# Choosing experts beside the gate tables: a re-staged slot schedule, 8-token one-hot compares, and the gate factor on ScalarE

## The chip, the core and the metric

The kernel runs on one core of one Trainium2 chip. The metric is the device time of one execution in microseconds (us); three runs of the kernel before gave 2725.94, 2727.11 and 2727.88, so the median is 2727.11. The engines are PE (TensorE), DVE (VectorE), ACT (ScalarE), POOL (GpSimd) and SP (SyncE, which here only issues transfers). Each has its own queue of instructions and takes them in order.

## What is computed

Two transformer blocks on 512 tokens of width 1024. The change lies in the expert layer that ends the first block. For every token and each of 8 heads, 16 of 16384 experts are chosen by two top-16 lists (one for each half of a key) and a top-16 over their sums; the expert's number is `i1 * 128 + i2`. In the reference:

```python
v1, i1 = lax.top_k(s1, PEER_TOPK_HALF)
v2, i2 = lax.top_k(s2, PEER_TOPK_HALF)
cand = (v1[..., :, None] + v2[..., None, :])...
top_s, pos = lax.top_k(cand, PEER_TOPK)
gate = jax.nn.softmax(top_s, axis=-1)
u = jnp.take(expert_u, experts, axis=0)
act = jax.nn.gelu(jnp.einsum('chkd,cd->chk', u, hc))
v = jnp.take(expert_v, experts, axis=0)
return jnp.einsum('chk,chkd->cd', gate * act, v)
```

## The kernel before

For the last 128 tokens the kernel gathers the chosen rows of `expert_u` and `expert_v` (128 choices of each) and works on them on DVE: "picks". For the first 384 tokens (tiles t = 0, 1, 2 of 128) it computes all 16384 experts densely in 128 blocks of 128, block i being one value of `i1`: a **U main** is `expert_u` block i times the activations (8 chunks of 3 matmuls, 128x384), gelu on ACT, and a store to a scratch tensor `asc`; a **V main** later multiplies gelu and gate with `expert_v` block i. Both split each weight block into a high part (`uhi`, an ACT copy, L100) and a remainder (`ulo`, a subtraction, L101).

The gate of every token and expert is a table built as a product of one-hot matrices: for each token, `ob` (128 choices x 128 values of i2) and `oa` (128 choices x 128 values of i1, times the gate) are multiplied on PE. `gate_rows` makes `ob` and `oa` for a **unit** of TB = 8 tokens, `gate_mm` multiplies them (8 products) into two PSUM banks and copies them to a staging tile `st`, which holds TG tokens. A full `st` is written to the scratch tensor `gsc` in 8 **pieces**. The V stage reads the table back (`vg`). 384 tokens are 48 units.

All of this is written under a hand-made order, in **slots**. Slot i issues the load of U block i+3, `u_prep(i+2)` (`uhi` on ACT, then `ulo` on the engine in `gb["ulo"]`), the caller's work for DVE, the U main i, the caller's `gate_mm`, gelu i, some pieces and some picks. Before the change the slots run in two stages one after the other:

- 25 slots with the choices (`choose`, a generator with seven parts, six of them each ahead of a slot) for the gathered tile and then tiles 0, 1, 2. `ulo` is on POOL here.
- 56 slots with the gates: seven units in eight slots, one pick in each. `ulo` is on DVE here. `gate_mm` of a unit runs in the slot after its `gate_rows`.

Five slots drain the pieces and two bridge to the U/V stage, where the last 40 blocks' U mains (U blocks 88 to 127) run among the 128 V mains. `choose` ends with an Exp on ACT (L611), which takes a change of the activation table and, at the next gelu, another. Buffers that matter: `uhi`, `ulo` and `uraw` three each, `ob` and `oa` two each, gate PSUM five banks, U main PSUM two.

Of the kernel before, what the change touches and what calls it, by code (L numbers as in the profile page):

```python
# [7 lines left out]
F32 = mybir.dt.float32  # L8
# [4 lines left out]
AF = mybir.ActivationFunctionType  # L13
ALU = mybir.AluOpType
# [6 lines left out]
P = 128  # L21
# [4 lines left out]
TD = 384  # L26
NH = 8
NE = 128
TB = 8
OB = 2  # L30
NTAP = 7
WINDOWS = (8, 15, 16, 17)
UPS = (7, 8)
TG = 64
IB = 16
CPICK, CGAP = (0, 1, 0, 0, 1, 0, 0), (1,)
BPICK, BDRAIN = 1, 2
BRIDGE = 2
MASK = -1.0e30
# [20 lines left out]
def body(nc, tc, A, out, stop=None):  # L60
# [23 lines left out]
    iotaf = const.tile([P, P], F32, name="iotaf")  # L84
# [193 lines left out]
    start = tc.manual_schedule()  # L278
# [17 lines left out]
    ps = lin.bank()  # L296
# [13 lines left out]
    first = [lin.bank() for _ in range(8)]  # L310
    H = []
    for k in range(DC):
        if k + 2 < DC:
            load(k + 2)
        h = tmp.tile([P, S], F32, tag="ht", name="ht", bufs=2)
# [7 lines left out]
        for m in range(8):  # L323
            j = m % 2 * P
# [36 lines left out]
    steps = [(mg, k0) for mg in order1 for k0 in (0, 4)]  # L361
# [19 lines left out]
    for i, (mg, k0) in enumerate(steps):  # L381
# [7 lines left out]
        if k0 == 0:  # L389
            ps = [lin.bank() for _ in range(2)]  # L390
# [21 lines left out]
    for c in range(4):  # L412
        ps = lin.bank()
# [4 lines left out]
                                       op1=ALU.subtract)  # L418
# [11 lines left out]
    ps = fsum(lin.bank(), ycv)  # L430
# [53 lines left out]
    GT = TD // P  # L484
# [8 lines left out]
    vvs = ExitStack()  # L493
# [199 lines left out]
        nc.scalar.copy(gb["t3"], pt)  # L693

    def gate_rows(t, q):
        if q == 0:
            gate_t(t)
        t3 = gb["t3"]
        ob = gp.tile([P, TB, P], F32, tag="ob", name="ob", bufs=OB)
        oa = gp.tile([P, TB, P], F32, tag="oa", name="oa", bufs=OB)  # L700
        for j in range(TB):
            of = lambda n: t3[:, n, q * TB + j:q * TB + j + 1]
            nc.vector.tensor_scalar(ob[:, j], iotaf, of(1), None, op0=ALU.is_equal)
            nc.vector.tensor_scalar(oa[:, j], iotaf, of(0), of(2), op0=ALU.is_equal, op1=ALU.mult)
        return t, q, ob, oa

    def gate_mm(t, q, ob, oa):

        g, o = divmod(t * P + q * TB, TG)
        if o == 0:  # L710
            gb["st"] = gp.tile([P, P, TG], F32, tag="st", name="st", bufs=2)
        for h in range(TB // 4):
            ps = pg.tile([P, 4, P], F32, tag="pg", name="pg", bufs=5)
            for j in range(4):
                nc.tensor.matmul(ps[:, j], ob[:, 4 * h + j], oa[:, 4 * h + j], start=True, stop=True)
            nc.scalar.copy(gb["st"][:, :, o + 4 * h:o + 4 * h + 4].rearrange("p i t -> p t i"), ps)
        if o + TB == TG:
            for b in range(NE // IB):
                pieces.append((Gsc[b][g], gb["st"][:, b * IB:(b + 1) * IB].rearrange("p i t -> p (i t)")))
# [12 lines left out]
    ui = 0  # L732

    def slot(dve=None, after=None, picks=0, drain=1):
        nonlocal ui
        i = ui
        ui += 1
        if i + 3 < NE:
            u_load(i + 3)
        u_prep(i + 2)  # L740
        r = dve() if dve else None
        u_main(i)
        if after:
            after()
        u_post(i, True)
        piece(drain)
        pick(picks)
        return r

    for n, t in enumerate([GT] + list(range(GT))):  # L750
        for n2, _ in enumerate(choose(t)):
            slot(picks=CPICK[n2] if n > 1 or n == 1 and n2 > 1 else 0)
    for n in CGAP:
        slot(picks=n)
    tk.close()
    vvs.close()
    gs = ExitStack()
    gp = R(gs, "gp")
    pg = pool(gs, "pg", 1, space=PSUM)
    units = [(t, q) for t in range(GT) for q in range(P // TB)]  # L760
    ready = []
    nu = 0
    first = ui
    gb["ulo"] = nc.vector
    while nu < len(units) or ready:
        mine = []
        want = (ui - first + 1) * UPS[0] // UPS[1]
        old, ready = ready, []

        def dve():  # L770
            nonlocal nu
            while nu < min(want, len(units)):
                ready.append(gate_rows(*units[nu]))
                nu += 1

        def after():
            for o in old:
                gate_mm(*o)
        slot(dve, after, 1)
    while pieces:  # L780
        slot(picks=BPICK, drain=BDRAIN)
    gs.close()
    gb["ulo"] = nc.gpsimd


# [8 lines left out]
    def v_load(i):  # L794
        raw = vp.tile([P, D], F32, tag="vraw", name="vraw", bufs=4)
        nc.sync.dma_start(raw, A["v"][i * P:(i + 1) * P, :])
        a = None
        kind = "s" if i in Asc else "d"
        if i % 2 == 0:
            VG[kind] = vp.tile([P, TD // TG, 2, TG], F32, tag=f"vg{kind}", name="vg", bufs=2 + (kind == "s"))  # L800
            o = i % IB * TG
            nc.sync.dma_start(VG[kind].rearrange("p g i t -> p g (i t)"),
                              Gsc[i // IB][:, :, o:o + 2 * TG].rearrange("g p n -> p g n"))
        g = VG[kind][:, :, i % 2]
        if i in Asc:
            a = vp.tile([P, TD], F32, tag="va", name="va", bufs=4)
            nc.sync.dma_start(a, Asc[i])
        V[i] = raw, g, a
# [23 lines left out]
                    hi[:, s2 * S:(s2 + 1) * S], lo[:, s2 * S:(s2 + 1) * S], nv == 0, nv == NE - 1)  # L832
        nv += 1

    if (ui + BRIDGE) % 2:
        slot(picks=BPICK)
    direct = list(range(ui + BRIDGE, NE))
    spilled = list(range(ui + BRIDGE))
# [420 lines left out]
```

## Time and profile before

| what | value |
|---|---|
| median of three runs | 2727.11 us (2725.94 to 2727.88) |
| the profiled execution | 2732.3 us, span 2730.5 us |
| PE, busy share of the span | 95% (weight loads 79%) |
| DVE / ACT / POOL | 72% / 36% / 29% |
| mean granted clock of TensorE | 0.977 |
| U mains 0 to 27 (choices) | 444.5 to 612.1 us |
| U mains 28 to 81 (gates) | to 923.2 us |
| U mains 82 to 87 (drain and bridge) | to 952.4 us |
| the U/V stage | to about 1660 us |
| DVE at the last top-16 lists of the query stage | to 455.8 us |

Busy times count an instruction from start to end; instructions of one engine overlap by a tenth of a microsecond or so, so the time that a run of them takes is read from start to start. A wait in brackets is the idle time of the engine just before the instruction and the instruction that ended it. PEclk is the granted clock, 1.0 being 2.4 GHz and 0.5 being 1.2 GHz.

### The profile page before, as it was taken

What the parts mean: (1) busy time and instruction counts of PE and PEld (TensorE: products, weight loads), DVE (VectorE), ACT (ScalarE), POOL (GpSimd) and SP (SyncE); (2) the same over time, 40 slices, a digit from 0 to 9 for tenths busy, and PEclk for the clock granted to TensorE, in tenths of its full rate; (3) what the DMA queues carried; (4) which work ended last, traced back from release to release, by engine and by line L of the source; (5) the groups of instructions that cost most, each with busy time, mean ns of one, the idle gap of its engine ahead of it and who ended that gap; (6) DMA issues with size and microseconds to landing.
All of it is one profiled execution on the core that took longest, in us unless ns stands there. A gap on an engine that the chain in (4) does not pass through costs nothing. (4 is left out here: it accounts for less than half of the span.)

```text
span 2730.5 us, 33539 instructions
## 1 busy us (share of the span) xinstructions
PE 2583.6 (95%) x12307; PEld 2153.1 (79%) x12307; DVE 1956.9 (72%) x3659; ACT 985.5 (36%) x1374; POOL 790.5 (29%) x455
## 2 busy tenths in 40 slices
PE   6988899769999999999999999999999999999998
PEld 4766679769999988887887887778888775788886
DVE  6999578999999688888888888644334475544433
ACT  3324333325555433333333335222232455422221
POOL 0000333542222377777777764000010000100000
PEclk8998999979999999999999999999999999999999
DMA  8434321437878899898989994222333221222232
GB/s 291 148 123 162 133 70 58 149 134 256 306 269 320 324 343 320 318 323 311 318 313 315 319 326 175 85 93 93 94 99 104 85 89 39 85 93 93 94 95 73
DMA packets 205061, 508.05 MB, mean 186 GB/s; under 512 B 18208, under 2 KB 94496, under 8 KB 204896
## 3 DMA queue, kind: packets, MB, share of 16 engines
q1 hardware_dynamic: 154928, 354.18, 37.6%
q0 software_dynamic: 36864, 134.23, 13.9%
q10 hardware_dynamic: 13104, 17.50, 1.8%
q8 instruction: 97, 1.59, 0.2%
q14 instruction: 68, 0.56, 0.1%
HBM read 461.23 MB, written 44.61 MB: 185 GB/s over the span
## 5 line engine op out<-in xcount | busy, mean ns | idle before, releaser
L101 DVE TENSOR_TENSOR wlo<-raw,whi 128x1024 fp32r<-128x1024 f32 x212 | 258.8, 1223 | 339.2 <-ACT whi L100 334.6
L100 ACT CAST whi<-raw 128x1024 fp32r<-128x1024 f32 x228 | 235.1, 1034 | 659.6 <-PE mm L105 547.5
L106 PE MATMUL act<-h2h,ulo 128*128 128x384 f32 x1024 | 348.8, 341 | 33.0 <-POOL ulo L101 25.6
L104 PE MATMUL act<-h2h,uhi 128*128 128x384 f32 x1024 | 351.8, 344 | 16.4 <-ACT ga L650 16.4
L105 PE MATMUL mm<-gl,whi 128*128 128x512 f32 x864 | 345.2, 400 | 3.6 <-DVE gl L208 3.5
L105 PE MATMUL act<-h2l,uhi 128*128 128x384 f32 x1024 | 347.2, 339 | 0.0
L104 PE MATMUL mm<-gh,whi 128*128 128x512 f32 x864 | 343.1, 397 | 0.4 <-DVE x L887 0.4
L106 PE MATMUL mm<-gh,wlo 128*128 128x512 f32 x864 | 342.0, 396 | 1.5 <-DVE wlo L101 1.5
L179 POOL TENSOR_TENSOR sq<-sq 128x512 f32<-128x512 f32 x24 | 37.0, 1542 | 960.9 <-ACT sq L173 960.3
L104 PE MATMUL pv<-vhi,ch 128*128 128x512 f32 x768 | 301.2, 392 | 7.2 <-ACT ch L821 7.2
L106 PE MATMUL pv<-vhi,cl 128*128 128x512 f32 x768 | 307.1, 400 | 0.0
L105 PE MATMUL pv<-vlo,ch 128*128 128x512 f32 x768 | 301.9, 393 | 5.3 <-POOL vlo L822 5.3
L680 POOL DMA_INDIRECT row<-in_u_dram,idx x128 | 185.3, 1448 | 297.3 <-DVE act L663 282.9
L106 PEld LDWEIGHTS act<-h2h,ulo 128*128 128x128 f32 x1024 | 195.8, 191 | 37.8 <-POOL ulo L101 29.8
L101 POOL TENSOR_TENSOR ulo<-uraw,uhi 128x1024 fp32r<-128x1024 f32 x68 | 193.1, 2842 | 100.9 <-ACT uhi L100 100.4
L104 PEld LDWEIGHTS act<-h2h,uhi 128*128 128x128 f32 x1024 | 196.0, 191 | 18.9 <-ACT ga L650 17.3
L671 DVE SCALAR_TENSOR_TENSOR gacc<-row,act,gacc 128x1024 f32<-128x1024 f32 x127 | 205.4, 1618 | 3.4 <-DMA row<-in_v_dram,idx 1.9
L105 PEld LDWEIGHTS mm<-gl,whi 128*128 128x128 f32 x864 | 162.5, 188 | 44.4 <-DVE gl L208 4.9
L105 PEld LDWEIGHTS act<-h2l,uhi 128*128 128x128 f32 x1024 | 196.1, 191 | 1.5
L104 PEld LDWEIGHTS mm<-gh,whi 128*128 128x128 f32 x864 | 162.4, 188 | 43.0 <-issue 2.3
L106 PEld LDWEIGHTS mm<-gh,wlo 128*128 128x128 f32 x864 | 162.5, 188 | 41.8 <-issue 2.0
L663 DVE CUSTOM_DVE_ANT_0 row<-row,h2t 128x1024 f32<-128x1024 f32 x128 | 178.4, 1405 | 13.2 <-DMA row<-in_u_dram,idx 13.2
(826 smaller groups left out, 5242.7 us busy)
## 6 DMA issues: line engine op xcount, KB each, us to landing
uraw<-in_uT_dram SPq DMA_DIRECT2D x128, 512.0 KB
vraw<-in_v_dram SPq DMA_DIRECT2D x128, 512.0 KB
raw<-in_w_in_dram SPq DMA_DIRECT2D x52, 512.0 KB
gsc<-st SPq DMA_DIRECT2D x48, 512.0 KB
vg<-gsc SPq DMA_DIRECT2D x64, 384.0 KB
raw<-in_ffn_w_gate_dram SPq DMA_DIRECT2D x44, 512.0 KB
raw<-in_ffn_w_up_dram SPq DMA_DIRECT2D x44, 512.0 KB
raw<-in_ffn_w_down_dram SPq DMA_DIRECT2D x40, 512.0 KB
```

Source lines behind the costliest of these rows:

```text
L100: nc.scalar.copy(hi, src)
L101: (lo_eng or nc.vector).tensor_sub(lo, src, hi.bitcast(F32))
L104: nc.tensor.matmul(ps, whi, ahi, start=first, stop=False)
L105: nc.tensor.matmul(ps, whi, alo, start=False, stop=False)
L106: nc.tensor.matmul(ps, wlo, ahi, start=False, stop=last)
L179: self.eng.tensor_add(self.acc, self.acc, t)
L663: nc.vector.tensor_tensor_reduce(out=r, in0=r, in1=h2t, scale=1.0, scalar=0.0, op0=ALU.mult, op1=ALU.add, accum_out=act[:, k:k + 1])
L671: nc.vector.scalar_tensor_tensor(gb["acc"], r, act[:, k:k + 1], gb["acc"], op0=ALU.mult, op1=ALU.add)
L680: nc.gpsimd.indirect_dma_start(out=r, out_offset=None, in_=A[table], in_offset=bass.IndirectOffsetOnAxis(ap=idx[:, k:k + 1], axis=0))
```

## The change

Five things are altered.

1. Choices and gates run in one loop of 82 slots (n = 0 to 81). The choices of the gathered tile and of tile 0 take two parts in every three slots up to n = 20; those of tiles 1 and 2 take one part in every third slot from n = 23 to 62. Units start at n = 22, three in four slots, and from n = 62 nine in ten. A tile's units wait in the program until its choice is complete. `ulo` is on DVE in all of the loop.
2. `gate_rows` makes `ob` and `oa` with one compare each for all 8 tokens (operands broadcast), not with 16 operations of one token; the gate factor is then multiplied into `oa`, in place, by 8 ACT operations of 128x128 with a per-partition scale.
3. `gate_mm` writes its products into PSUM with the token as the innermost index (each matmul's 128 columns lie 16 bytes apart), so that the copy to `st` reads the bank in order and writes runs of 4 values, where it wrote single values 256 bytes apart.
4. `st` holds 32 tokens, not 64: 96 pieces of 256 KB with up to two issued in a slot, where there were 48 of 512 KB with one. `vg` is loaded for four blocks at a time (768 KB), not two (384 KB), with two buffers of each kind.
5. Fewer picks ahead of the U/V stage: 58 rather than 67. The number of slots ahead of it stays 86 and two of the bridge.

```diff
-UPS = (7, 8)
-TG = 64
+TG = 32
+GI = 4
 IB = 16
-CPICK, CGAP = (0, 1, 0, 0, 1, 0, 0), (1,)
...
         ob = gp.tile([P, TB, P], F32, tag="ob", name="ob", bufs=OB)
         oa = gp.tile([P, TB, P], F32, tag="oa", name="oa", bufs=OB)
+        k0 = q * TB
+        shape = [P, TB, P]
+        row = lambda n: t3[:, n, k0:k0 + TB, None].to_broadcast(shape)
+        cols = iotaf[:, None, :].to_broadcast(shape)
+        nc.vector.tensor_tensor(ob, cols, row(1), op=ALU.is_equal)
+        nc.vector.tensor_tensor(oa, cols, row(0), op=ALU.is_equal)
         for j in range(TB):
-            of = lambda n: t3[:, n, q * TB + j:q * TB + j + 1]
-            nc.vector.tensor_scalar(ob[:, j], iotaf, of(1), None, op0=ALU.is_equal)
-            nc.vector.tensor_scalar(oa[:, j], iotaf, of(0), of(2), op0=ALU.is_equal, op1=ALU.mult)
+            nc.scalar.activation(oa[:, j], oa[:, j], AF.Copy, scale=t3[:, 2, k0 + j:k0 + j + 1])
         return t, q, ob, oa
...
         for h in range(TB // 4):
-            ps = pg.tile([P, 4, P], F32, tag="pg", name="pg", bufs=5)
+            ps = pg.tile([P, P, 4], F32, tag="pg", name="pg", bufs=5)
             for j in range(4):
-                nc.tensor.matmul(ps[:, j], ob[:, 4 * h + j], oa[:, 4 * h + j], start=True, stop=True)
-            nc.scalar.copy(gb["st"][:, :, o + 4 * h:o + 4 * h + 4].rearrange("p i t -> p t i"), ps)
+                nc.tensor.matmul(ps[:, :, j], ob[:, 4 * h + j], oa[:, 4 * h + j], start=True, stop=True)
+            nc.scalar.copy(gb["st"][:, :, o + 4 * h:o + 4 * h + 4], ps)
...
-    for n, t in enumerate([GT] + list(range(GT))):
-        for n2, _ in enumerate(choose(t)):
-            slot(picks=CPICK[n2] if n > 1 or n == 1 and n2 > 1 else 0)
-    for n in CGAP:
-        slot(picks=n)
-    tk.close()
-    vvs.close()
...
+    gens = [choose(t) for t in torder]
     ready = []
-    nu = 0
-    first = ui
+    steps = nu = n = 0
     gb["ulo"] = nc.vector
     while nu < len(units) or ready:
-        mine = []
-        want = (ui - first + 1) * UPS[0] // UPS[1]
+        csteps = 2 * (n + 1) // 3 if n < 21 else min(28, 14 + (n - 20) // 3)
+        want = max(0, (n - 20) * 3 // 4) if n < 62 else 32 + (n - 62) * 9 // 10
         old, ready = ready, []
 
         def dve():
-            nonlocal nu
-            while nu < min(want, len(units)):
+            nonlocal nu, steps
+            while steps < csteps:
+                next(gens[steps // 7], None)
+                steps += 1
+            while nu < min(want, len(units), max(0, steps // 7 - 1) * (P // TB)):
                 ready.append(gate_rows(*units[nu]))
                 nu += 1
...
-        slot(dve, after, 1)
+        slot(dve, after, 0 if n < 11 or n % 4 == 3 and n < 62 or n % 3 != 2 and n < 21 else 1, 2)
+        n += 1
     while pieces:
         slot(picks=BPICK, drain=BDRAIN)
...
-            VG[kind] = vp.tile([P, TD // TG, 2, TG], F32, tag=f"vg{kind}", name="vg", bufs=2 + (kind == "s"))
...
+            vg = VG[kind, i // GI] = vp.tile([P, TD // TG, GI, TG], F32, tag=f"vg{kind}", name="vg", bufs=2)
...
-    if (ui + BRIDGE) % 2:
+    while (ui + BRIDGE) % GI:
         slot(picks=BPICK)
```

The queue of ACT before, in the middle of the gate stage (`uhi`: split of a U block; `st<-pg`: copy of a gate bank; `ga`: gelu; `asc`: store of it):

```order
L100 CAST uhi<-uraw 128x1024
L716 COPY st<-pg 128x4x128 x2
L650 ACTIVATE ga<-act 128x384
L654 DMA asc_6867<-ga 128x384
L100 CAST uhi<-uraw 128x1024
```

The same queue now, in a slot of the loop that has a unit and follows one that has (`oa<-oa`: the gate factor), up to the next split:

```order
L99 CAST uhi<-uraw 128x1024
L708 ACTIVATE oa<-oa,t_5608 128x128 x8
L720 COPY st<-pg 128x128x4 x2
L649 ACTIVATE ga<-act 128x384
L653 DMA asc_5759<-ga 128x384
L99 CAST uhi<-uraw 128x1024
```

Between the split of one block and the split of the next, eight operations on this slot's `oa` now stand ahead of the copies of the unit before.

The queue of DVE before, in the gate stage (`row`, `act`: a pick; `ob`, `oa` stand here once of eight times on either side):

```order
L704 TENSOR_SCALAR oa<-iotaf,t_4664 128x128
L663 ISA row,act<-row,h2t 128x1024
L663 ISA act 128x1
L101 TENSOR_TENSOR ulo<-uraw,uhi 128x1024
L703 TENSOR_SCALAR ob<-iotaf,t_4664 128x128
L704 TENSOR_SCALAR oa<-iotaf,t_4664 128x128
```

The same queue now, in a slot that has a unit and a part of the choices (`x`, `I_3307`: that part):

```order
L100 TENSOR_TENSOR ulo<-uraw,uhi 128x1024
L562 TENSOR_TENSOR x<-x 128x128x8
L562 TENSOR_TENSOR x<-x 128x128x4
L562 TENSOR_TENSOR x<-x 128x128x2
L563 TENSOR_TENSOR I_3307<-x 128x128
L599 TENSOR_TENSOR x<-ge,starts 128x2048
L705 TENSOR_TENSOR ob<-iotaf,t_4325 128x1024
L706 TENSOR_TENSOR oa<-iotaf,t_4325 128x1024
L662 ISA row,act<-row,h2t 128x1024
L662 ISA act 128x1
L100 TENSOR_TENSOR ulo<-uraw,uhi 128x1024
```

The remainder `ulo` comes first, then the part of the choices, then the two compares, then the pick.

## Rows read from the trace of the kernel before

**Rows 1.** Windows by stage: length, busy PE, PEld, DVE, ACT, POOL, PEclk, DMA, GB/s

```profile
444.50:612.10 167.60, 128.71 (x694) 126.26 (x693) 162.76 (x481) 56.05 (x72) 78.06 (x32) 0.88 0.42 137
612.10:923.20 311.10, 311.10 (x2072) 311.10 (x2072) 296.11 (x917) 172.82 (x207) 87.20 (x55) 1.00 0.80 282
...
952.40:1660.00 707.60, 686.54 (x3156) 575.70 (x3155) 611.72 (x558) 239.13 (x326) 512.03 (x290) 1.00 0.91 320
```

**Rows 2.** Waits from 444.5 to 612.1: waiting, releaser, us in total, times, longest

```profile
ACT ex L611 <- DVE ex L585: 31.9, 3, 12.8
...
PE act L106 <- POOL ulo L101: 16.7, 3, 15.5
```

**Rows 3.** Timeline of PE in the gate stage: start, us, engine, line, operation, tiles

```profile
709.78 1.95 PE L715 MATMUL pg<-oa,ob 128*128 128x128 f32 x16
711.48 0.42 PE L104 MATMUL act<-h2h,uhi 128*128 128x384 f32 x1
...
717.43 0.42 PE L104 MATMUL act<-h2h,uhi 128*128 128x384 f32 x1
```

**Rows 4.** Timeline of PE: first matmuls of U mains 2 and 3, back to back

```profile
454.71 0.33 PE L104 MATMUL act<-h2h,uhi 128*128 128x384 f32 x1
...
458.87 0.33 PE L104 MATMUL act<-h2h,uhi 128*128 128x384 f32 x1
```

**Rows 5.** Timeline of DVE through one slot of the gate stage

```profile
703.17 1.21 DVE L663 CUSTOM_DVE_ANT_0 row<-row,h2t 128x1024 f32<-128x1024 f32 x1
...
704.31 1.22 DVE L101 TENSOR_TENSOR ulo<-uraw,uhi 128x1024 fp32r<-128x1024 f32 x1
...
705.45 0.28 DVE L703 TENSOR_SCALAR ob<-iotaf,t 128x128 f32<-128x128 f32 x1
...
709.07 1.21 DVE L663 CUSTOM_DVE_ANT_0 row<-row,h2t 128x1024 f32<-128x1024 f32 x1
```

**Rows 6.** Timelines of DVE (the choice of tile 2) and of POOL

```profile
572.62 0.29 DVE L570 CAST IF<-II 128x256 bf16<-128x256 uint32 x1
...
587.56 3.12 DVE L595 TENSOR_TENSOR x<-x,IF 128x2048 bf16<-128x2048 bf16 x1
...
603.40 0.29 DVE L619 TENSOR_TENSOR GA<-ex,sm 128x128 f32<-128x128 f32 x1
...
584.56 5.05 POOL L101 TENSOR_TENSOR ulo<-uraw,uhi 128x1024 fp32r<-128x1024 f32 x2
```

**Rows 7.** Timelines of ACT: two gate copies; gelu and the next split; a table load

```profile
664.75 2.03 ACT L716 COPY st<-pg 128x512 f32<-128x512 f32 x2 [2.07 <-PE pg L715]
...
521.37 0.50 ACT L650 ACTIVATE ga<-act 128x384 f32<-128x384 f32 x1 [2.16 <-PE act L106]
...
522.32 1.06 ACT L100 CAST uhi<-uraw 128x1024 fp32r<-128x1024 f32 x1 [0.45 <-ACT ga L650]
...
530.59 1.28 ACT L611 ACT_TABLE_LOAD   x1 [0.40 <-ACT ga L650]
```

**Rows 8.** Timelines of ACT and DVE: a split, and the remainder that waited for it

```profile
927.69 1.05 ACT L100 CAST uhi<-uraw 128x1024 fp32r<-128x1024 f32 x1 [4.00 <-DMA uraw<-in_uT_dram]
...
928.77 1.23 DVE L101 TENSOR_TENSOR ulo<-uraw,uhi 128x1024 fp32r<-128x1024 f32 x1 [4.33 <-ACT uhi L100]
```

**Rows 9.** Timelines of ACT: a 128x128 operation and its successor; a 128x512 copy and its

```profile
2183.76 0.40 ACT L1078 ACTIVATE s__17856<-s__17856,st__17857 128x128 f32<-128x128 f32 x1 [0.40 <-DVE st__17857 L1077]
2184.07 0.19 ACT L1078 ACTIVATION_READ_ACCUMULATOR s__17856<-s__17856,st__17857 128x1 f32 x1
...
418.46 0.59 ACT L537 COPY q<-mm 128x512 f32<-128x512 f32 x1 [3.89 <-PE mm L106]
418.95 1.05 ACT L100 CAST whi<-raw 128x1024 fp32r<-128x1024 f32 x1
```

**Rows 10.** Timeline of PE: the matmul after an idle time, and one 3.5 us later

```profile
57.37 0.79 PE L105 MATMUL mm<-hl,whi 128*128 128x512 f32 x1 [2.62 <-DVE hl L196]
...
60.87 0.40 PE L104 MATMUL mm<-hh,whi 128*128 128x512 f32 x1
```

More of the change, by code (lines that the diff above doesn't have):

```diff
@@ L782, in body @@
     gs.close()
+    tk.close()
+    vvs.close()
     gb["ulo"] = nc.gpsimd
@@ L798, in v_load @@
         kind = "s" if i in Asc else "d"
-        if i % 2 == 0:
-            VG[kind] = vp.tile([P, TD // TG, 2, TG], F32, tag=f"vg{kind}", name="vg", bufs=2 + (kind == "s"))
[L801 to L804, printed above, removed]
+        if (kind, i // GI) not in VG:
+            for k in [k for k in VG if k[0] == kind]:
+                del VG[k]
+            vg = VG[kind, i // GI] = vp.tile([P, TD // TG, GI, TG], F32, tag=f"vg{kind}", name="vg", bufs=2)
+            o = i // GI * GI % IB * TG
+            nc.sync.dma_start(vg.rearrange("p g i t -> p g (i t)"),
+                              Gsc[i // IB][:, :, o:o + GI * TG].rearrange("g p n -> p g n"))
+        g = VG[kind, i // GI][:, :, i % GI]
         if i in Asc:
```

## The prediction, made before the changed kernel ran

> **What bounds the kernel now.** I read the windows by stage first. Two stages lie ahead of the U/V stage. In the first (choices), DVE is busy 162.8 of 167.6 us and PE only 128.7, at a mean granted clock of 0.88; in the second (gates), PE is busy all of 311.1 us and DVE 296.1 [rows 1]. So the first is bound by DVE and the second by PE, with DVE close behind. The waits of the first stage show how DVE reaches PE: ACT sits at the Exp that ends a choice until DVE has come to that choice (31.9 us in three waits), and PE then lacks its remainder `ulo` [rows 2]. In the gate stage a slot takes 5.95 us from one U main to the next, of which the gate products take 1.7 to 1.8 (711.48 less 709.78) [rows 3]; a bare U main takes 4.16 [rows 4], so I count 1.79 for a unit's products. DVE's slot there is 1.14 for `ulo`, 3.62 for the 16 one-hot operations and 1.14 for the pick, 5.90 in all [rows 5].
>
> If only sums of work counted, merging the stages would pay: PE has 88 U mains of 4.16 and 48 units of 1.79, 452 us, and takes 508 now (444.5 to 952.4).
>
> **What the change costs DVE.** Sixteen operations (3.62) become two 128x1024 compares. The nearest row is the 128x1024 f32 subtraction, 1.22 long and 1.14 from start to start [rows 5]; it too reads two f32 operands. So 2.28 for a unit. The choice of tile 2 took 31.0 us (572.62 to 603.69) [rows 6], with two picks in it (2.3) and two remainders on POOL, 5.05 us, beside which a 2048-element operation took 3.12 [rows 6]. I take 4 off for that and call a choice alone 25 us: six long parts of 4.0 and a short last one of 1.0. `ulo` comes to DVE in the first stage too, 1.14 a slot. In slots 0 to 21 that makes 1.14 + 2 x 25 / 21 = 3.5 a slot, under PE's 4.16. In all, DVE would have about 100 (choices) + 109 (units) + 96 (`ulo`) + 60 (picks) = 365 us. No engine's sum is near 508.
>
> **What the change makes ACT and DVE wait for.** This term decides. Both queues are taken in order, and in a slot with a unit they now read: ACT `uhi`, 8 gate factors, 2 gate copies, gelu, store; DVE `ulo`, the choice's part if there is one, `ob`, `oa`, pick. `ulo` waits for this slot's `uhi`. The factors wait for this slot's `oa`, which stands behind `ulo`. The next `uhi` stands behind the factors, the copies and the gelu. That is a closed relay with nothing overlapped but the pick. Before, ACT's part held no wait for this slot's DVE work: its copies waited for the PE products of the unit before. Round the relay once:
>
> - `uhi` to the start of `ulo`: 1.08 [rows 8];
> - `ulo` and `ob`, start to start: 1.14 each; `oa` to its end: 1.22 [rows 5];
> - 8 factors at 0.31: a 128x128 ACT operation with a per-partition operand took 0.40 and its successor began 0.31 after it [rows 9]: 2.48;
> - 2 gate copies at 0.49: before, two took 2.03, about 0.93 a copy with its scattered writes [rows 7]; a 128x512 copy out of PSUM with neighbouring writes holds ACT for 0.49 [rows 9]. The new writes are runs of four values. I take 0.49: 0.98;
> - gelu and store up to the next `uhi`: 0.95 [rows 7].
>
> Together 9.0 us, against 5.95 for PE. The Trainium skill's page Advanced Engine Details and Errata, section SBUF Cachelines, says that accesses within one 16-byte line run at full speed, which is just such a run of four; no row here shows it, and by it the copy's lower end would hold.
>
> PE keeps up: it has two slots of prepared weights in hand. It will idle about 3 us a slot, and after 2.62 us of idling a matmul took 0.79, back at 0.40 some 3.5 us later [rows 10], so about 1.8 us is lost to the 1.2 GHz clock: 5.95 + 1.8 = 7.7, still under 9.0.
>
> **The sum.** In the order of the slots:
>
> - U mains 0 and 1 as before, to 454.9. `ulo` of block 2 must wait for DVE's last top-16 of the query stage, which ends at 455.8 (table), and takes 1.14: about 2 us. Slots 2 to 21: 20 x 4.16 = 83. With a little slow clock, 541.
> - Slots 22 to 61: ten groups of four, three with a unit. The fourth holds `uhi` 0.96, the copies left over 0.98 and the 0.95, 2.9 in all, and spares the slot after it its copies: 3 x 9.0 + 2.9 - 1.0 = 28.9, ten times 289. Ten long parts of choices lie in slots with a unit, in the relay between `ulo` and `ob`: 40. Two lie in slots without, where DVE needs 1.14 + 4.0 + 1.14 = 6.3 against 2.9: 7. The Exp at slot 41 brings two table loads of 1.28 [rows 7], 2.9 with itself. Together 339, to 880.
> - Slot 62 (two units, a short part, an Exp): 9.0 - 1.0 + 2.3 + 1.0 + 2.9 = 14; slot 63: 4. To 898.
> - Slots 64 to 80, 16 units and one slot without: 16 x 9.0 + 2.9 - 2 x 1.0 = 145, to 1043. The last unit's products end about there too, and U mains 82 to 87 take 25, with one more us for loads: 1069.
>
> Before, U main 87 ended at 952.4. The change is +117 us: the profiled execution would go from 2732.3 to about 2849, and against the median of 2727.1, which is 5 less, the time is **2844 us**.
>
> **The other edits.** The wait for an Exp goes (the 31.9 above), as its input is made five parts earlier and DVE no longer lags; that is in the sum, since slots 0 to 21 run at PE's pace. In the U/V stage nine more picks fall on DVE, some 12 us; it is idle 96 of 707.6 us there [rows 1], and I take nothing. `vg` comes in 32 loads of 768 KB rather than 64 of 384 KB; the extra 384 KB ahead of another load takes 1.2 us at 320 GB/s [rows 1], and loads go out four jobs ahead, some 16 us. Cover gone, it costs 32 x 1.2 = 38. The smaller pieces move the same bytes, and slots that grow longer ask less of the queues: SP's loads of U blocks, which stand behind pieces that wait for ACT's copies, have 9 us now rather than 6. On POOL the remainders are gone and the picks stay. I take nothing for these.
>
> **Bounds.** The compare has one near row. A factor is between 0.12 (the share of 128 columns in the 0.49 of 512) and its whole 0.40, which moves the relay by -1.5 or +0.7; a copy between 0.49 and 0.93 moves it by up to +0.9. So the relay is 7.5 to 10.6, and 48 units of it are -72 to +77 us: 2772 to 2921.
>
> **Rivals.**
>
> *The queues slide past each other (faster).* PE stays the bound throughout: 452 us of work, some 8 for the first `ulo`, transposes and loads, 460 against 508: 48 less, 2679. It needs a relay below 5.95; the whole change breaks even where 48 units save 117, at a relay of 9.0 - 2.4 = 6.6. For it speaks that no engine's sum comes near. The Trainium skill's page Perfetto Trace Analysis, section Optimization Strategy, says that stages with different busiest engines may gain from being interleaved; that is this change, and by it this rival would hold. Against it stands the order of both queues, and that the compares, one `ulo`, `uhi` and gelu alone, all with near rows, are 5.5 without a factor or a copy. Chance 5%.
>
> *The products get slow.* Each matmul now writes its 128 columns 16 bytes apart. No row shows such a write. The relay hides the products up to 9.0 - 4.16 = 4.8 us a unit, more than 2.5 times today's. At four times, 7.2, PE needs 366 + 346 + 8 = 720 for what takes 508: 2939. The Trainium skill's page Advanced Engine Details and Errata, section PSUM Cachelines, says that outputs which are not contiguous slow matmuls down considerably, without a factor; no run before shows it. Chance 8%.
>
> *The U/V stage starves* on the larger loads with its DMA share already at 0.91 [rows 1]: 2844 + 38 = 2882. Chance 7%.
>
> **How the numbers follow.** The forecast has 80%. The range leaves out the first two rivals and the tails of the bounds: 2785 to 2905. A difference of 0.2% is about what a measurement of this kernel can tell from none. Faster by more than that 5%, within it 1%, slower 94%.
>
> **What would show it.** Right: from slot 22 on, U mains about 9 us apart in slots with a unit and 13 where a part of a choice lies in them; ACT's largest wait being for `oa`, DVE's for `uhi`; PE idle a third of the time, its granted clock below 1 there; slots 2 to 21 4.16 apart without a wait; the U/V stage within 5 us of 707.6. Wrong: units' slots under 7 us, products over 4 us a unit, or PE waits in the U/V stage above today's 21 us.

## The result, and the profile of the changed kernel

| | median | runs | profiled execution |
|---|---|---|---|
| before | 2727.49 us | 2725.94 to 2729.08 (4) | 2732.3 us, span 2730.5 |
| after | 2842.65 us | 2841.7 to 2847.72 (4) | 2842.34 us, span 2840.6 |

The ratio is 1.0426, with a 95% interval of 1.0408 to 1.0444: the change costs 115 us. The forecast was 2844.

**Where the time went.** The windows of the changed kernel ahead of the U/V stage, cut at slots 0 to 22, the slots in which choices and units share DVE, the slots with units alone, and the drain (columns as in [rows 1]):

```profile
444.50:540.00 95.50, 95.50 (x554) 95.47 (x553) 85.42 (x274) 40.59 (x53) 5.01 (x5) 1.00 0.57 189
540.00:898.00 358.00, 280.80 (x1561) 268.97 (x1560) 209.32 (x366) 178.40 (x421) 32.39 (x33) 0.91 0.52 175
898.00:1041.00 143.00, 115.00 (x657) 107.53 (x656) 75.76 (x83) 77.87 (x188) 15.92 (x17) 0.99 0.60 205
1041.00:1066.00 25.00, 24.78 (x140) 23.82 (x139) 11.28 (x14) 7.53 (x11) 12.95 (x8) 1.00 1.04 376
```

In the first row PE is never idle: the choices no longer hold it up, as they did in [rows 1]. In the second and third, 501 us together, no engine is full: PE 396 us, DVE 285, ACT 256. That is the mark of engines waiting for each other. Before, PE was busy in all of the gate stage.

The U/V stage is nearly as it was. The last V product ends at 1685.4 in the kernel before, not at the "about 1660" of the table, and at 1797.1 in the changed one. From U main 88 to there, before and then after:

```profile
952.25:1685.38 733.13, 712.07 (x3267) 596.49 (x3267) 633.57 (x580) 251.18 (x342) 519.38 (x293) 1.00 0.89 315
```

```profile
1061.08:1797.09 736.01, 714.76 (x3267) 594.29 (x3267) 645.08 (x598) 251.07 (x342) 535.43 (x302) 1.00 0.92 321
```

That is 2.9 us more for the same 3267 matmul records.

The waits from 540 to 1045 (waiting, releaser, us in total, times, longest), the largest ones of ACT, DVE and PE:

```profile
DVE ulo L100 <- ACT uhi L99: 214.0, 58, 5.4
ACT oa L708 <- DVE oa L706: 212.4, 47, 8.7
...
PE pg L719 <- ACT oa L708: 80.8, 38, 8.3
```

ACT waits for DVE and DVE for ACT, some 213 us each way, about 4.4 for each of the 48 units. One turn of this, from ACT's timeline (start, us, engine, line, operation, tiles; in brackets the idle time before, and what ended it):

```profile
950.77 1.05 ACT L99 CAST uhi<-uraw 128x1024 fp32r<-128x1024 f32 x1 [0.40 <-ACT ga L649]
955.38 2.45 ACT L708 ACTIVATE oa<-oa,t 128x128 f32<-128x128 f32 x8 [3.56 <-DVE oa L706]
957.74 1.04 ACT L720 COPY st<-pg 128x512 f32<-128x512 f32 x2
958.68 0.49 ACT L649 ACTIVATE ga<-act 128x384 f32<-128x384 f32 x1
...
959.56 1.05 ACT L99 CAST uhi<-uraw 128x1024 fp32r<-128x1024 f32 x1 [0.40 <-ACT ga L649]
```

and from DVE's, the same turn:

```profile
951.85 1.23 DVE L100 TENSOR_TENSOR ulo<-uraw,uhi 128x1024 fp32r<-128x1024 f32 x1 [4.16 <-ACT uhi L99]
953.00 1.22 DVE L705 TENSOR_TENSOR ob<-iotaf,t 128x1024 f32<-128x1024 f32 x1
954.13 1.22 DVE L706 TENSOR_TENSOR oa<-iotaf,t 128x1024 f32<-128x1024 f32 x1
955.26 1.22 DVE L662 CUSTOM_DVE_ANT_0 row<-row,h2t 128x1024 f32<-128x1024 f32 x1
...
960.65 1.22 DVE L100 TENSOR_TENSOR ulo<-uraw,uhi 128x1024 fp32r<-128x1024 f32 x1 [4.16 <-ACT uhi L99]
```

Read the starts in one line: `uhi` 950.77, `ulo` 951.85, `ob` 953.00, `oa` 954.13, factors 955.38, copies 957.74, gelu 958.68, next `uhi` 959.56. From one `uhi` to the next are 8.79 us, and at every moment of them one of the two engines works for the other. The pick lies beside the factors and costs nothing. PE's timeline of the same turn:

```profile
950.43 0.44 PE L103 MATMUL act<-h2h,uhi 128*128 128x384 f32 x1 [0.84 <-ACT ga L649]
...
955.84 2.54 PE L719 MATMUL pg<-oa,ob 128*128 128x128 f32 x16 [0.97 <-ACT oa L708]
...
959.22 0.44 PE L103 MATMUL act<-h2h,uhi 128*128 128x384 f32 x1 [0.84 <-ACT ga L649]
```

PE's U mains are 8.79 us apart, too: PE follows, waiting once for the factors and once for the gelu.

### The profile page after: what moved, and what is told of

Same layout as the page of the kernel before. It is cut to its first block, busy times and chain, and to the rows that moved or that the text cites. A ratio compares the mean times of both kernels' runs of the same rounds, so it can differ in the third digit from the quotient of the medians.

```text
span 2840.6 us, 33250 instructions
## 1 busy us (share of the span) xinstructions
PE 2632.9 (93%) x12307; PEld 2181.3 (77%) x12307; DVE 1880.0 (66%) x3012; ACT 1054.3 (37%) x1758; POOL 692.7 (24%) x430
## 4 chain that ended last, share of the span: by engine, by line
PE 61%; DVE 15%; ACT 9%; issue 8%; DMA 3%; POOL 3%; ACTq 1%; SPq 0%; DVEq 0%; POOLq 0%
PE mm L104 13%; PE mm L103 13%; PE mm L105 13%; ACT oa L708 4%; PE pv L105 3%; PE pv L104 3%; PE pv L103 3%; PE act L105 3%; PE act L103 3%; PE act L104 3%; DVE ycv L335 2%; POOL row L679 2%; DVE oa L706 2%; DVE ob L705 2%; ACT uhi L99 2%
## 5 line engine op out<-in xcount | busy, mean ns | idle before, releaser
L679 POOL DMA_INDIRECT row<-in_u_dram,idx x128 | 149.5, 1168 | 593.7 <-DVE act L662 518.5
L100 DVE TENSOR_TENSOR ulo<-uraw,uhi 128x1024 fp32r<-128x1024 f32 x85 | 103.8, 1223 | 229.8 <-ACT uhi L99 229.8
L719 PE MATMUL pg<-oa,ob 128*128 128x128 f32 x768 | 131.7, 334 | 80.8 <-ACT oa L708 80.8
L708 ACT ACTIVATE oa<-oa,t 128x128 f32<-128x128 f32 x384 | 117.4, 388 | 212.4 <-DVE oa L706 212.4
```

What stands on the lines that cost most here:

```text
L100: (lo_eng or nc.vector).tensor_sub(lo, src, hi.bitcast(F32))
L679: nc.gpsimd.indirect_dma_start(out=r, out_offset=None, in_=A[table], in_offset=bass.IndirectOffsetOnAxis(ap=idx[:, k:k + 1], axis=0))
L708: nc.scalar.activation(oa[:, j], oa[:, j], AF.Copy, scale=t3[:, 2, k0 + j:k0 + j + 1])
L719: nc.tensor.matmul(ps[:, :, j], ob[:, 4 * h + j], oa[:, 4 * h + j], start=True, stop=True)
```

## The experiments

Theory A is the prediction's: the time is the closed chain through the two queues taken in order. Its rivals: theory D, that merging the choices into the gates' slots and staging by 32 tokens cost the time by themselves; theory C, that the products became slow because they write PSUM in strides. In the diffs the context is the changed kernel unless said otherwise. Each ratio is against the kernel before, with its 95% interval.

**1. The factors one slot later.**

```diff
 def gate_rows(t, q):
-        for j in range(TB):
-            nc.scalar.activation(oa[:, j], oa[:, j], AF.Copy, scale=t3[:, 2, k0 + j:k0 + j + 1])
-        return t, q, ob, oa
+        return t, q, ob, oa, t3
...
 def dve():
...
+            for o in old:
+                gate_factor(*o)
```

`gate_factor` holds the 8 removed operations, and `old` is the unit of the slot before.

> The changed kernel, with one thing moved: the 8 gate factors of a unit stand on ScalarE one slot later, behind the next uhi, where their oa was finished a slot before. Nothing is added or taken away. Theory A (the relay: ScalarE's factors wait for this slot's oa, oa stands behind ulo on VectorE, ulo waits for this slot's uhi, and the next uhi stands behind the factors): the relay is open, a unit's slot goes from 8.8 us to what ScalarE or PE need by themselves, 6.0 to 6.7; 48 units at 2.1 to 2.8 less are 100 to 135 us, so 2705 to 2745. Theory D (taking the choices into the gates' slots and staging by 32 tokens cost the time by themselves) and theory C (products that write PSUM in strides): within 20 us of 2842.

Measured: 2703.45 us, ratio 0.9907 (0.989 to 0.9923). ACT's timeline now:

```profile
811.24 1.05 ACT L99 CAST uhi<-uraw 128x1024 fp32r<-128x1024 f32 x1 [0.40 <-ACT ga L649]
812.19 2.44 ACT L711 ACTIVATE oa<-oa,t 128x128 f32<-128x128 f32 x8
...
817.19 1.05 ACT L99 CAST uhi<-uraw 128x1024 fp32r<-128x1024 f32 x1 [0.40 <-ACT ga L649]
```

The 3.56 us ahead of the factors are gone and a slot takes 5.95 us, PE's own time. No operation was saved: 139 us were the place of 8 operations in a queue. D and C fall as causes of the loss: all that they blame is still in this kernel.

**2. The factor on VectorE.**

```diff
-        for j in range(TB):
-            nc.scalar.activation(oa[:, j], oa[:, j], AF.Copy, scale=t3[:, 2, k0 + j:k0 + j + 1])
+        nc.vector.tensor_mul(oa, oa, row(2))
```

> The changed kernel, with the 8 gate factors taken from ScalarE and done as one 128x1024 multiplication on VectorE, right behind the compare. ScalarE then waits for nothing that VectorE does in the same slot. Theory A: the relay is open; VectorE has 1.14 x 5 = 5.7 us in a slot with a unit and 4 more in every fourth, PE 4.16 and 1.8 to 2.5, so a group of four slots takes 22 to 24.5 us rather than 32, and the total is 2690 to 2745. Theories C and D: within 20 us of 2842.

Measured: 2725.44 us, 0.9988 (0.9978 to 0.9998), in the upper half of A's range. The waits from 540 to 900 show what is last now:

```profile
ACT st L719 <- PE pg L718: 157.7, 87, 7.4
...
PE pg L718 <- DVE oa L707: 30.3, 14, 5.1
```

ACT has no factors left and no longer waits for `oa`; its largest wait is now for PE. PE waits for DVE in the slots that hold a part of a choice, where U mains stand 9 to 13 us apart. The relay is open: 117 us come back. The 22 us that are missing against experiment 1 lie in these slots, where DVE has 1.14 more for a unit.

**3. The new rows in the stages of before** (context: the kernel before).

```diff
-        for j in range(TB):
-            of = lambda n: t3[:, n, q * TB + j:q * TB + j + 1]
-            nc.vector.tensor_scalar(ob[:, j], iotaf, of(1), None, op0=ALU.is_equal)
-            nc.vector.tensor_scalar(oa[:, j], iotaf, of(0), of(2), op0=ALU.is_equal, op1=ALU.mult)
...
+        nc.vector.tensor_tensor(ob, cols, row(1), op=ALU.is_equal)
+        nc.vector.tensor_tensor(oa, cols, row(0), op=ALU.is_equal)
+        for j in range(TB):
+            nc.scalar.activation(oa[:, j], oa[:, j], AF.Copy, scale=t3[:, 2, k0 + j:k0 + j + 1])
```

> The kernel before with its two stages, its contiguous PSUM rows and its staging by 64 tokens; only the one-hot rows are the changed ones: two compares on VectorE and 8 factors on ScalarE for a unit. Theory A: the same relay closes in the gate stage, now with the copies of before (0.93 rather than 0.47): 8.8 + 0.9 = 9.7 us for a slot with a unit, 48 of them and 7 slots of some 4 without, so the gate stage goes from 311 us to 480 to 500 and the total to 2890 to 2920. Theory D: VectorE gets 1.3 us a unit back and ScalarE has room, so 2715 to 2735.

Measured: 2886.99 us, 1.0581 (1.0564 to 1.0599), 3 us below A's range. The choice stage is as it was. The gate stage went from 311.1 us [rows 1] to 468 (612.1 to 1079.8, where U main 82 starts), 12 us less than the 480 to 500 that I had expected of it. ACT's timeline in it:

```profile
798.98 1.05 ACT L100 CAST uhi<-uraw 128x1024 fp32r<-128x1024 f32 x1 [0.40 <-ACT ga L650]
803.60 2.45 ACT L708 ACTIVATE oa<-oa,t 128x128 f32<-128x128 f32 x8 [3.56 <-DVE oa L706]
805.95 1.86 ACT L720 COPY st<-pg 128x512 f32<-128x512 f32 x2
...
808.52 1.05 ACT L100 CAST uhi<-uraw 128x1024 fp32r<-128x1024 f32 x1 [0.40 <-ACT ga L650]
```

The same turn, 9.54 us: the relay came with the rows, not with the merged order.

**4. The strided products alone** (context: the kernel before).

```diff
-            ps = pg.tile([P, 4, P], F32, tag="pg", name="pg", bufs=5)
+            ps = pg.tile([P, P, 4], F32, tag="pg", name="pg", bufs=5)
...
-                nc.tensor.matmul(ps[:, j], ob[:, 4 * h + j], oa[:, 4 * h + j], start=True, stop=True)
-            nc.scalar.copy(gb["st"][:, :, o + 4 * h:o + 4 * h + 4].rearrange("p i t -> p t i"), ps)
+                nc.tensor.matmul(ps[:, :, j], ob[:, 4 * h + j], oa[:, 4 * h + j], start=True, stop=True)
+            nc.scalar.copy(gb["st"][:, :, o + 4 * h:o + 4 * h + 4], ps)
```

> The kernel before with one thing changed: the products write their PSUM columns 16 bytes apart, and the copy reads and writes in the same order. 16 rows of products took 1.79 us before and 2.54 in the changed kernel. If the writes in strides are the cause, a unit costs PE 0.75 us more here too, and the gate stage, bound by PE, grows by 36 us: about 2763. If the products are paced by the factors that ScalarE makes beside them (0.295 us each, two rows for each), they stay at 1.8 here and the total at 2720 to 2730. Theory C in its full form (products several times slower) expects 2840 and above. In each case ScalarE's copies should go from 0.93 to 0.47 us.

Measured: 2729.21 us, 1.0004 (0.9995 to 1.0014). The costliest groups of lines from 636 to 898 (line, engine, operation, tiles, shapes, count; busy us, mean ns of one; idle before):

```profile
L716 ACT COPY st<-pg 128x512 f32<-128x512 f32 x79 | 46.4, 587 | 111.1 <-PE pg L715 111.1
```

```profile
L715 PE MATMUL pg<-oa,ob 128*128 128x128 f32 x631 | 76.9, 275 | 0.0
```

The trace has two records for each product, 16 for a unit. Their mean length is 275 ns with the columns 16 bytes apart, and 275 in the kernel before, without strides; but the ends of matmuls are modelled in the profile, so the starts decide. These are 0.111 us apart in both kernels, and from U main 28 to U main 82 both take 309.4 us. So the 2.54 us that the 16 records took in the changed kernel are no slow writes: they ran beside the factors that they needed. And in experiment 1, where the factors are ready in good time, the 16 records took 1.95, the 1.95 of [rows 3]. Theory C falls. The copies are shorter but hidden behind PE, and the total does not move.

**5. The chain cut at its other link.** ScalarE's order is untouched; on VectorE `ulo` goes behind the compares.

```diff
-        split(hi, lo, U[i][0], gb["ulo"])
+        nc.scalar.copy(hi, raw)
+        r = dve() if dve else None
+        gb["ulo"].tensor_sub(lo, raw, hi.bitcast(F32))
```

> The changed kernel with ScalarE's order as it was, the 8 factors in the slot of their oa; on VectorE alone, ulo of a slot is put behind the choice's part and the unit's two compares rather than ahead of them. No instruction is added or taken away. Theory A: the compares no longer wait for this slot's uhi, so the relay is cut at its other link; a slot with a unit falls to PE's pace of 6 us where no part of a choice lies in it, and the total to 2700 to 2750. If it is the amount of work on ScalarE that sets the slot, and not the order across the two queues, the slots stay at 8.8 us and the total at 2830 to 2850.

Measured: 2704.73 us, 0.9918 (0.9901 to 0.9934). ACT's and DVE's timelines:

```profile
815.48 1.04 ACT L638 CAST uhi<-uraw 128x1024 fp32r<-128x1024 f32 x1 [0.40 <-ACT ga L653]
816.43 2.45 ACT L712 ACTIVATE oa<-oa,t 128x128 f32<-128x128 f32 x8
...
820.61 1.04 ACT L638 CAST uhi<-uraw 128x1024 fp32r<-128x1024 f32 x1 [0.40 <-ACT ga L653]
```

```profile
819.98 1.22 DVE L710 TENSOR_TENSOR oa<-iotaf,t 128x1024 f32<-128x1024 f32 x1
821.69 1.23 DVE L640 TENSOR_TENSOR ulo<-uraw,uhi 128x1024 fp32r<-128x1024 f32 x1 [0.49 <-ACT uhi L638]
```

`oa` is begun before `uhi` is, so the factors stand ready to go behind it, and ACT's turn takes 5.13 us here, its own work, which is less than PE's 5.95. Two cuts at different places of one cycle, each moving nothing but order, give the same time. That speaks for the cycle, and against ScalarE's amount of work as the cause: all of that work is in both kernels.

**6. Half of the factors.**

```diff
-        for j in range(TB):
+        for j in range(0, TB, 2):
```

> The changed kernel with only every second of the 8 gate factors; half of the rows are left without their gate value. Theory A: the relay loses four steps of 0.295 us, 1.18 us, in each of 48 units and nothing else moves: slots of 7.6 us rather than 8.8, and 57 us less, 2775 to 2795. If ScalarE's time is not in the chain the total stays within 20 us of 2842; if the first factor is what holds the chain (a wait, not its length), it does so too.

Measured: 2791.89 us, 1.0238 (1.0221 to 1.0255). ACT's timeline:

```profile
915.14 1.05 ACT L99 CAST uhi<-uraw 128x1024 fp32r<-128x1024 f32 x1 [0.40 <-ACT ga L649]
919.75 1.28 ACT L708 ACTIVATE oa<-oa,t 128x128 f32<-128x128 f32 x4 [3.56 <-DVE oa L706]
...
922.79 1.05 ACT L99 CAST uhi<-uraw 128x1024 fp32r<-128x1024 f32 x1 [0.41 <-ACT ga L649]
```

The turn went from 8.79 to 7.65, by 1.14 for four steps of 0.295, and the wait for `oa` is still 3.56. 48 units of 1.14 are 55 us; 51 were measured. The length of the factors is in the chain at full price.

**7. The merged order with the old rows.** The code of `gate_rows` is that of before (the removed lines of experiment 3); the rest is the changed kernel.

> The changed kernel (choices beside the gates, staging by 32 tokens, four blocks to a load, products in strides) with the one-hot rows made as before: 16 operations on VectorE that apply the factor too, nothing on ScalarE. Theory A: no relay; VectorE has 5.9 us in a slot with a unit and about 23 in a group of four, so the total is 2695 to 2740. Theory D (the merged order or the finer staging cost by themselves): 2820 and above.

Measured: 2701.03 us, 0.9907 (0.9891 to 0.9924). Its window (columns as above):

```profile
540.00:898.00 358.00, 354.73 (x2215) 342.89 (x2214) 346.86 (x1115) 150.96 (x224) 79.97 (x50) 1.00 0.72 256
```

PE and DVE are both all but full in the slots where the changed kernel left PE idle for 77 us. PE's busy time counts products that keep the pace of DVE's rows (16 records in 3.19 us at 549.16, against 1.95 where the rows are ready). With experiments 3 and 7 the change comes apart into its two halves:

| us | DVE rows of before | compares, factors on ACT |
|---|---|---|
| two stages of before | 2727.5 | 2887.0 |
| merged, staged by 32, products strided | 2701.0 | 2842.65 |

The merge, with the staging, the loads and the picks that came with it, gains 26 us with the old rows. The new rows lose 142 to 160 in either order. Theory D has the wrong sign.

**8. Factors late, and the compares ahead of the choice's part.** The diff of experiment 1, and this:

```diff
 def dve():
+            while nu < min(want, len(units), max(0, steps // 7 - 1) * (P // TB)):
+                ready.append(gate_rows(*units[nu]))
+                nu += 1
             while steps < csteps:
                 next(gens[steps // 7], None)
                 steps += 1
-            while nu < min(want, len(units), max(0, steps // 7 - 1) * (P // TB)):
-                ready.append(gate_rows(*units[nu]))
-                nu += 1
```

> The changed kernel with the factors one slot later, as in the first experiment, and the unit's two compares put ahead of the choice's part on VectorE instead of behind it. With the factors late alone, slots that hold a part of a choice took 6.8 to 10 us where others took 6.0, because oa came too late even for the next slot. Theory A with the order of VectorE as what is left: these slots fall to 6.0 too, some 20 of them at 1 to 1.5 us each, so 2675 to 2695. If VectorE's amount of work is what is left, within 5 us of 2703.

Measured: 2696.39 us, 0.9887 (0.9871 to 0.9904): 7 us less than experiment 1, whose interval overlaps this one. It is 1.4 above A's range and 1.6 below that of the rival, so neither was met. Most slots with a part fell to 6.0, but a few stayed at 9 to 10, and ACT's timeline at one of them (10.3 us) names something else:

```profile
634.51 1.04 ACT L99 CAST uhi<-uraw 128x1024 fp32r<-128x1024 f32 x1 [4.93 <-DMA uraw<-in_uT_dram]
635.46 2.44 ACT L711 ACTIVATE oa<-oa,t 128x128 f32<-128x128 f32 x8
```

Here `uhi` waits for its block to arrive, and factors whose input is ready stand behind it.

**9. The compares ahead of the choice's part, factors not late.** The diff of experiment 8, without that of experiment 1.

> The changed kernel with one thing moved on VectorE: the unit's two compares stand ahead of the choice's part in a slot, not behind it; the factors stay in the same slot as their compare. The prediction put ten long choice parts of 4.0 us into the relay, 40 us. Theory A: the relay stays closed at 8.8 us, but the part of the choice now lies beside the factors, the copies, the gelu and the next uhi (5.2 us together), so slots with a part fall from 11 to 13 us to about 9, and the total by 30 to 40 us, to 2802 to 2815. If VectorE's amount of work in these slots counts and not its place, within 10 us of 2842.

Measured: 2810.46 us, 1.0299 (1.0282 to 1.0316). A slot with a part, DVE and then ACT:

```profile
637.65 1.23 DVE L100 TENSOR_TENSOR ulo<-uraw,uhi 128x1024 fp32r<-128x1024 f32 x1 [3.20 <-ACT uhi L99]
...
641.06 1.57 DVE L562 TENSOR_TENSOR x<-x 128x1024 bf16<-128x1024 bf16 x3
...
646.45 1.23 DVE L100 TENSOR_TENSOR ulo<-uraw,uhi 128x1024 fp32r<-128x1024 f32 x1 [0.80 <-ACT uhi L99]
```

```profile
641.18 2.45 ACT L708 ACTIVATE oa<-oa,t 128x128 f32<-128x128 f32 x8 [3.56 <-DVE oa L706]
...
649.98 2.44 ACT L708 ACTIVATE oa<-oa,t 128x128 f32<-128x128 f32 x8 [3.56 <-DVE oa L706]
```

The relay is closed, at 8.80, but the choice's part (641.06 to 645.6) now lies beside ACT's half of it. 32 us came back, inside the range, against the 40 that the prediction had put there.

**10. The old PSUM layout and the scattered copy in the changed kernel.** The diff of experiment 4, backwards.

> The changed kernel with the products written to PSUM side by side and the copy writing its SBUF rows scattered, as before the change. The copy's own time on ScalarE goes from 0.47 to about 0.93 us, two to a unit, and stands in the relay. Theory A: 0.92 us more in each of 48 units, 44 us, so 2880 to 2892. Theory C (the strided products hold the kernel up): faster than 2842. If ScalarE's copies are hidden, within 10 us of 2842.

Measured: 2878.61 us, 1.0548 (1.0531 to 1.0566). ACT:

```profile
948.65 1.85 ACT L720 COPY st<-pg 128x512 f32<-128x512 f32 x2
950.31 0.51 ACT L649 ACTIVATE ga<-act 128x384 f32<-128x384 f32 x1
```

Two copies hold ACT for 1.66, not the 1.86 that I had reckoned, against 0.94 in order: 0.72 a unit, a turn of 9.55, and 36 us rather than 44, which leaves the total 1.4 under the range. The same edit that was worth nothing in experiment 4 is worth 36 us where the copies are in the chain.

**11. Old rows, ahead of the choice's part.** Experiment 7 with the reordering of experiment 8.

> The changed kernel with the 16 one-hot operations of before on VectorE (factor in them, nothing on ScalarE) and the unit's operations ahead of the choice's part in a slot. With these operations behind the part, some 14 slots that hold one took 7 to 9 us where others took 5.95. Theory A: what is left of the lost time is the order of VectorE, so these slots fall to 6 us, 15 to 20 us in all: 2680 to 2692. If VectorE's amount of work is what is left (22.8 us in a group of four slots, against PE's 22.0), within 6 us of 2701.

Measured: 2694.57 us, 0.9872 (0.9855 to 0.9888), the lowest median of all (its interval overlaps that of experiment 8) and 1.3% under the kernel before, yet a miss: 6.5 us gained on experiment 7 and not 15 to 20. In its window

```profile
540.00:898.00 358.00, 353.39 (x2244) 344.66 (x2243) 346.94 (x1118) 151.56 (x226) 83.81 (x51) 1.00 0.75 261
```

DVE is busy 347 of 358 us, as in experiment 7: its amount of work fits what was left, and little remained for order to win. No run took work off DVE there, so this is a reading of the window and not a test. Late blocks are a second reading: ACT's `uhi` waited for its block 20.1 us there, in nine waits.

**12. The factors late and ahead of `uhi`.** Experiment 8 with the factors of the unit before as the first thing that a slot puts on ACT.

```diff
+        if pre:
+            pre()
         u_prep(i + 2)
...
+        def pre():
+            for o in old:
+                gate_factor(*o)
...
```

> The changed kernel with the compares ahead of the choice's part and the factors one slot later, and now ahead of that slot's uhi on ScalarE rather than behind it. With the factors behind uhi, two slots of 9 to 10 us were left where uhi waited almost 5 us for its block from memory and the factors, whose input was ready, stood behind it. Theory A: queue order again; the factors no longer share that wait, 5 to 10 us less than 2696, so 2685 to 2693. If the load itself is what PE waits for, within 3 us of 2696.

Measured: 2725.78 us, 0.9994 (0.9984 to 1.0004): 29 us worse than experiment 8, where I had expected a gain or no change. The timelines say why:

```profile
821.82 2.45 ACT L711 ACTIVATE oa<-oa,t 128x128 f32<-128x128 f32 x8 [2.22 <-DVE oa L706]
824.18 1.03 ACT L99 CAST uhi<-uraw 128x1024 fp32r<-128x1024 f32 x1
...
828.78 2.44 ACT L711 ACTIVATE oa<-oa,t 128x128 f32<-128x128 f32 x8 [2.22 <-DVE oa L706]
```

```profile
825.25 1.23 DVE L100 TENSOR_TENSOR ulo<-uraw,uhi 128x1024 fp32r<-128x1024 f32 x1 [2.32 <-ACT uhi L99]
...
827.53 1.22 DVE L706 TENSOR_TENSOR oa<-iotaf,t 128x1024 f32<-128x1024 f32 x1
```

A second, shorter relay: factors 821.82, `uhi` 824.18, `ulo` 825.25, `oa` 827.53, next factors 828.78, in all 6.96 us, over PE's 5.95. Having the factors a slot late isn't enough; `uhi` must stand ahead of them, so that DVE's turn starts before theirs. I had not walked that cycle before the run. The waits for late blocks did fall, as far as the waits from 540 to 1000 show it, from 25 us in ten to 12 in four, but that is small beside it.

## Why the prediction was right

**The relay.** Forecast 9.0 us, measured 8.79. Link by link, forecast and start-to-start time of the turn above: `uhi` to `ulo` 1.08 and 1.08; `ulo` 1.14 and 1.15; `ob` 1.14 and 1.13; `oa` to the first factor 1.22 and 1.25; eight factors 2.48 and 2.36; two copies 0.98 and 0.94; gelu to `uhi` 0.95 and 0.88. Each price was taken from a row of the same operation or of another one of like shape, and none was off by more than 0.12. Experiments 1 and 5 show that it is a cycle, 6 and 10 that its links count at full price, and 3 that it belongs to the new rows.

**The sum.** From U main 2 to the end of U main 87, the forecast had 614 us (454.7 to 1069), the trace 610.3 (450.8 to 1061.1), the kernel before 497.5 (454.7 to 952.25). Slots 22 to 61 took 336 against 339 forecast, slots 62 and 63 15.7 against 18, and slots 64 to 81, with the last products, 149 against 145. U mains of slots 2 to 20 stood 4.16 us apart, and those over a slot with a unit and a part of a choice 10.2 to 16.0, where the forecast had 13 (the longest also holds a late block, see below). Ahead of slot 22, one step failed: the 2 us for the `ulo` of block 2. U main 2 started 4.16 us after U main 1 without a wait; the remainders of blocks 0 to 2 had been made between 327.9 and 333.5, and the one that DVE made behind the last lists of the query stage, at 451.9, was block 3's.

**A term put at nothing, and one that covered it.** For late U blocks the prediction took nothing. In the slots of the loop ACT's `uhi` waited three times for its block, 3.35, 3.90 and 4.24 us, each time behind a slot without a unit, whose turn on ACT is short (2.8 us from the `uhi` at 564.91 to the next). The last of the three:

```profile
975.03 1.05 ACT L99 CAST uhi<-uraw 128x1024 fp32r<-128x1024 f32 x1 [4.24 <-DMA uraw<-in_uT_dram]
```

This wait is about what slots 64 to 81 took too long. The two others lie in slots 22 to 61, whose sum held all the same, because there the relay was 0.2 us a unit shorter than forecast and the choices' parts cheaper (below). That part of the agreement is luck. Why the blocks came late was not tested.

**An offset that did not come back.** I took 5 us off, because the profiled execution of before lay that far above its median. Its first U main began at 444.5; in the profiled runs of all kernels here it began between 439.3 and 444.5, in the changed one at 440.6. So some 4 of those 5 us lay ahead of everything that the change touches. The changed kernel's profiled run agrees with its median within 0.3 us. For it the sum gave 2849 and 2842.3 was measured: 3.9 by the earlier start, 4 by the sum, less about 1 behind it. That the total came within 2 us owes something to this correction and to errors of both signs in the sum; each of its stretches was good to about 4.

**PE.** The products took 2.54 us and not 1.79, which I did not foresee: they start with the first factor and keep the factors' pace. It was free, since the relay hides it. PE's idle time is therefore smaller than I said: 105 us of the 501 in the two windows, a fifth and not a third, 1.81 us in a turn and not 3. My 1.8 us a slot for the slow clock did not arise there: with two waits of 0.97 and 0.84 us a turn the granted clock was 0.99 (898 to 1041). It was 0.91 from 540 to 898, where PE waits up to 8.3 us for factors behind a part of a choice. Neither moved the time, as PE was not the bound: from 540 to 1045 ACT waited for PE once, for 0.2 us.

**The choices' parts.** Forecast 40 us in the relay; experiment 9, which takes them out of it, gained 32. That sets the worth of their place, near the term's size but below it.

**What I called free.** The U/V stage took 736.0 us against 733.1, and PE's waits in it came to 21 us in both. The larger `vg` loads, which took 9.6 us from issue to landing, and the nine picks more, which show as 11.5 us more of DVE, cost at most these 2.9 together; the third rival, a stage that starves, did not happen. Whether the smaller pieces have a part in the late blocks was not tested.

**The rivals.** Not one of them happened. The first, queues that slide past each other, needed a relay under 5.95 us; experiments 1, 5 and 7 show what the kernel looks like when the relay is open: PE at 5.95 a slot and 2701 to 2705 us, not the 2679 I had worked out. Most of the difference lies in the slots with a choice's part: some 13 of them took 7 to 9 us in experiment 7, about 23 us over 5.95, and that rival's sum had left them out. The Trainium skill's page Perfetto Trace Analysis, section Optimization Strategy, says that interleaving stages whose busiest engines differ may improve performance. Experiment 7 agrees (26 us gained); in the changed kernel the order of two queues undid it. The second rival fell with experiment 4: the Trainium skill's page Advanced Engine Details and Errata, section PSUM Cachelines, says that an access which is not contiguous slows matmuls markedly; here the records of 128x128 f32 products with columns 16 bytes apart started 0.111 us apart, and 0.111 without strides, so the measurement decides against it for this shape and type. The Trainium skill's page Advanced Engine Details and Errata, section SBUF Cachelines, says that accesses which hit one 16-byte line run at full performance; the copies agree: 0.47 us each with runs of four values, 0.83 with scattered ones.

## What to carry to other kernels

When work moves from one in-order engine to another, sums of busy time do not tell the cost: write both queues of one slot side by side, follow each wait to what stands ahead of its releaser, and if the walk comes back to its start, the slot takes the sum of the links. To open such a cycle it is enough to let one link use the result of the slot before, but walk the new order too, for a shorter cycle may be in it (6.96 us in experiment 12). An edit's worth hangs on whether it lies in the cycle: the same copy, 0.83 or 0.47 us long, made no difference behind PE and one of 36 us in the relay.

## What the runs showed of the hardware

- 128x128 f32 products that write PSUM columns 16 bytes apart ran at the pace of contiguous ones: 0.111 us from record to record (two records for each product), and a ratio of 1.0004 for the whole kernel.
- Waits of 0.97 and 0.84 us in every 8.79 left the granted clock at 0.99; it was 0.91 in the stretch with waits of up to 8.3 us.
- A 128x128 ACT operation with a per-partition factor is 388 ns long and lets the next one start 295 ns after it, eight in 2.36 us.
- A 128x512 copy from PSUM to SBUF held ACT for 0.47 us where four neighbouring values are written at a time, and for 0.83 where each value is written apart.
